# A two-layer transformer on one core: the first feed-forward part's second product by seven products for eight, a fourth raw weight buffer, and token sums held until h

## The chip, the cores and the metric

One core of a Trainium2 chip runs the whole forward pass. The metric is device time in microseconds (us), as the median of several runs of one launch. Engine names: PE is TensorE, DVE is VectorE, ACT is ScalarE, POOL is GpSimd, SP is SyncE (here it only issues DMAs).

## The reference, cut to what matters

Each of two layers takes x (512 tokens by 1024) through three steps, each closed by a layer norm: a feed-forward half step, a token mix (three kinds of attention with gates), and a second feed-forward half step. The change lies in the feed-forward parts, of which there are four in all:

```python
def _swiglu(x, w1, w2):
    gt, up = jnp.split(x @ w1, 2, axis=-1)      # w1: 1024 x 5632
    return (jax.nn.silu(gt) * up) @ w2          # w2: 2816 x 1024
...
x = _layer_norm(DN_ALPHA * x + 0.5 * _swiglu(x, ffn1_w1[l], ffn1_w2[l]), ln1_g[l], ln1_b[l])
```

All data are fp32. The kernel gets fp32 accuracy by three matmuls for one: each operand is split into a high part and a rest (ACT copies the high part `hi`, DVE subtracts to get `lo`), and hi·hi, hi·lo and lo·hi are summed in PSUM.

## The kernel before, in words

**Order of the work.** The program is one stream: FFN part 1 (layer 0, first half step), mix, part 2, part 3, mix, part 4. PE and POOL run in the order in which the code is written (`manual_schedule`). DVE, ACT and SP are ordered by a scheduler when the program is built, and run in that fixed order; an instruction that waits holds everything behind it on its engine.

**First product of a part.** The 2816 features are 22 blocks of 128, `f` = 0 to 21. For f from 4 on, `strassen(f, seven(w1, f))` makes gate and up of a block by seven products for eight: 7 products of 12 matmuls of 256 columns, 84 matmuls per f, into the PSUM tiles `pg`, `pu`, `pv`. `seven` loads two raw weight tiles by SP (L422, L423), sums and differences of them go into `ws` (DVE, L429 to L432), which are split like the weights (L438, L439), and a half tile into `dh`, `dl` (L440, L441). `strassen` copies `pg` to `sn` on ACT (L525) in the middle of the block; PE's later matmuls into `pg` wait for that copy. A last DVE operation on `pg` (L537) and a silu on ACT (L473) make h, kept in `ha` (blocks 0 to 17) and `hb` (18 to 21). The raw tiles rotate through the pool `wt`, 3 buffers. The tokens' own sums (`token_sums`, five DVE groups on x, then splits into `th`, `tl`) are made once per part, while blocks 2 and 3 run.

**Second product of a part.** h (512 by 2816) times w2 (2816 by 1024). In parts 2, 3 and 4 `strassen_rows` takes pairs of feature blocks, 9 pairs (`NS = 9`), and makes each pair's eight block products by seven: a first pass of four products (24 matmuls of 512 columns per pair), merges on DVE, then a second pass of three (18 matmuls per pair); the last 4 blocks (`NTAIL`) are plain, 24 matmuls per block. In part 1 `rows_ln` makes all 22 blocks plainly, 24 matmuls of 512 columns per block. The h of a pair is split and summed by `s_parts` (L491 on): single blocks into `sh`, `sl` (ACT L483, DVE L484, 128x256), differences `s` (L495, L498), their split (L483, L484, 128x768: three tiles in one instruction), and a last difference into `ha` (L503).

**Sums of w2.** The seven products need sums of w2's quarters, `ts` with four planes t1 to t4. `weight_sums` builds them in DRAM by software DMAs that POOL issues (L397), 768 KB each, plain copies and copies that add into the target, 8 per group of 3 pairs. They are taken off a queue one at a time by `sums_step`, which first copies one column of some fresh tile on POOL (L408, `pace`) so that a step does not start before that tile exists. Before the change this happens in the mixes only; part 1 has no `ts` (its first entry is `None`). In part 1's first product POOL also copies bias rows (`bvec`, L436), each behind a copy of a column of `ws` (L435).

Of the kernel before, what the change touches and what calls it, by code (L numbers as in the profile page):

```python
# [64 lines left out]
def body(tc, a, out, depth=DEPTH):  # L65
# [37 lines left out]
    peT = const.tile([P, depth, 2, 32], F32, name="peT")  # L103
    stats = [const.tile([P, 8], F32, name=f"st{i}") for i in range(NB)]
    pace = const.tile([P, 48], F32, name="pace")
    pace, pace2 = pace[:, 0:1], pace[0:64, 16:17]

    xh = xtp.tile([P, KD, S], F32R, name="xh")
    xl = xtp.tile([P, KD, S], F32R, name="xl")
# [4 lines left out]


    extra = K()
    extra.pool, extra.n = None, 0

    def wraw(shape=None):
        extra.n += 1  # L120
        if extra.pool and extra.n % 5 < 2:
            return extra.pool.tile([P, KD, P], F32, name="raw", tag="raw", bufs=2)
        return wt.tile(list(shape or [P, KD, P]), F32, name="raw", tag="raw", bufs=3)

    more = K()
    more.pool, more.n = None, 0
# [138 lines left out]

    def strassen_rows(w2, ts, sp, plain, ln, clear, nxt, tmp):


        def acc8():
            return [ps(name="acc") for _ in range(8)]  # L270
# [11 lines left out]
        a1 = acc8()  # L282
        for p in range(NS):
            if p == 2:
                extra.pool = rp
            rb, ra = wraw(), wraw()
            nc.sync.dma_start(flat(rb)[:, 0:512], w2[2 * p * P:(2 * p + 1) * P, 0:512])
            nc.sync.dma_start(flat(rb)[:, 512:1024], ts[:, p, 1024:1536])
            nc.sync.dma_start(flat(ra), ts[:, p, 0:1024])
            sh, sl = sp(p)  # L290
            ub, ua = wsplit(rb), wsplit(ra)
            prods = [(0, 0, ub, lo4), (1, 3, ub, hi4), (2, 1, ua, hi4), (3, 2, ua, lo4)]
            for i, j, w, c in prods[:1] + prods[2:] + prods[1:2] if p == 0 else prods:
                for b in range(2):
                    mm(a1[2 * i + b], (sh[:, j], sl[:, j]), w, b, c, p == 0, p == NS - 1)
# [34 lines left out]
        for p in range(NS):  # L330
            uc, d, dc = weights(p)
            sh, sl = sp(p, True)
            prods = [(0, 1, uc, lo4), (1, 0, uc, hi4), (2, 2, d, dc)]
            for i, j, w, c in prods[2:] + prods[:2] if p == NS - 1 else prods:
                for b in range(2):
                    mm(a2[2 * i + b], (sh[:, j], sl[:, j]), w, b, c, p == 0, False)
            if p in (1, 2):
                merge(p - 1)
        rest = []
        for k in range(2 * NS, KF):  # L340
            rest.append((k, plain(k), wrows(w2, k)))
        extra.pool.release()
        extra.pool = None
        clear()
        nx.pool = pool("nx", reuse_waits="tile")
        ln.scale_rows()
# [31 lines left out]
        return pts  # L378

    NTAIL = 4  # L380
    NS = 9
    NG = 3
    sums = deque()

    def weight_sums(w2):


        ts = dram.tile([P, NS, 2048], F32, name="ts", tag="ts", bufs=3)
        n = NS // NG

        def step(g, i):
            c = slice(n * g, n * g + n)
            v = w2[2 * n * g * P:2 * n * (g + 1) * P].rearrange("(q two p) f -> two p q f", two=2, p=P)
            b11, b12, b21, b22 = (v[j][:, :, 512 * k:512 * k + 512] for j in range(2) for k in range(2))
            t1, t3, t2, t4 = (ts[:, c, 512 * k:512 * k + 512] for k in range(4))
            o, x = ((t1, b11), (t3, b12), (t2, b22), (t1, b12), (t4, b21), (t3, b22), (t2, t1), (t4, t2))[i]
            nc.gpsimd.dma_start(o, x, **({"accum_op": OP.add} if i in (3, 5, 6, 7) else {}))  # L397

        for g in range(NG):
            sums.extend(lambda g=g, i=i: step(g, i) for i in range(8))  # L400
        return ts

    def sums_step(t, psum=False):
# [40 lines left out]
    def token_sums(st):  # L444


        x = st.ha[:, 10:18]
        th, tl = (st.w1p.tile([P, 4, 4, 256], F32R, name=n) for n in ("th", "tl"))
        t = [y[:, i:i + 2].rearrange("p a (b s) -> p (a b) s", b=2) for y, i in
             ((st.hb, 0), (st.hb, 2), (st.ha, 6), (st.ha, 8))]  # L450
        tt = nc.vector.tensor_tensor
        for i in range(0, KD, 2):
            c = slice(i, i + 2)
            tt(x[:, c], xh[:, c].bitcast(F32), xl[:, c].bitcast(F32), op=OP.add)
        p_, q, r_, s_ = x[:, 0:4, 0:256], x[:, 0:4, 256:512], x[:, 4:8, 0:256], x[:, 4:8, 256:512]
        for i, u, v in ((0, q, p_), (1, s_, t[0]), (2, s_, q), (3, r_, t[1])):
            tt(t[i], u, v, op=OP.subtract)
        for i in range(4):
            nc.scalar.activation(th[:, i], t[i], AF.Copy)
            tt(tl[:, i], t[i], th[:, i].bitcast(F32), op=OP.subtract)  # L460
        st.t = [(th[:, i], tl[:, i]) for i in range(4)]

    def ffn(l, w1, w2, which, xap, xa, wts, pend, done_prev, last, nxt, ts):
# [4 lines left out]
        def hpart(f):  # L468
            return (st.ha, st.hb)[f >= NA][:, f - NA * (f >= NA)]

        def evac(f, pg, pu):
            t = st.lnp.tile([P, S], F32, name="t", tag="t", bufs=3)
            nc.scalar.activation(t, pg, AF.Silu)  # L473
            nc.vector.tensor_tensor(hpart(f), t, pu, op=OP.mult)

        made, hs = {}, {}

        def h_parts(k, t):
            parts(t[:, 0], t[:, 1], hpart(k))
            hs[k] = t  # L480

        def parts(hi, lo, x):
            nc.scalar.activation(hi, x, AF.Copy)  # L483
# [24 lines left out]
        def strassen(f, ws):  # L508
            (ug, u1, u2, ud), (t1, t2, t3, t4) = ws, st.t
            ga, pa, pb = ps(name="pg"), ps(name="pu"), ps(name="pv")  # L510
            p_, r_, s_ = [(xh[:, k:k + 4, c], xl[:, k:k + 4, c]) for k, c in ((0, H1), (4, H1), (4, H2))]

            def prod(o, w, k0, x, first=True):
                for k in range(4):
                    hi, lo = w[0][:, k0 + k], w[1][:, k0 + k]
                    vh, vl = x[0][:, k], x[1][:, k]
                    for i, (wx, vx) in enumerate(((hi, vh), (hi, vl), (lo, vh))):
                        nc.tensor.matmul(o, wx, vx, start=first and k == 0 and i == 0, stop=k == 3 and i == 2,  # L518
                                         skip_group_check=True)

            tt = nc.vector.tensor_tensor
            prod(ga[:, H1], ug, 0, p_)
            prod(ga[:, H2], u1, 0, t1, False)
            sn = st.w1p.tile([P, S], F32, name="sn", tag="sn", bufs=2)
            nc.scalar.activation(sn, ga, AF.Copy)  # L525
# [12 lines left out]
            evac(f, ga, u)  # L538

        pts = staged(wts, pend)  # L540
        for tb in range(NB):
# [7 lines left out]
        st.ha = fa.tile([P, NA, S], F32, name="ha")  # L549
        st.w1p = nx.w1 = pool("w1p", side="right", reuse_waits="tile")  # L550
        more.n = 4
        evac(0, pts[0], pts[1])
        evac(1, pts[2], pts[3])
        for f in range(2, KF):
            if f == KF - 1 and ts is None:
                for k, n in enumerate(("hi", "lo")):
                    h_parts(k, wt.tile([P, KD, P], F32R, name=n, tag=n, bufs=3)
                            .rearrange("p (a b) c -> p a (b c)", a=2))
            elif f == KF - 1:
                w = [wt.tile([P, KD, P], F32R, name=n, tag=n, bufs=3).rearrange("p (a b) c -> p a (b c)", a=4)  # L560
                     for n in ("hi", "lo")]
                v, sn = (st.w1p.tile([P, 2, 256], F32, name=n, tag=n, bufs=2) for n in ("v", "sn"))
# [18 lines left out]
        ln = LN(hsp, which, l, xa, 0.5, last, ts is not None)  # L581

        def wload(k):
            if k not in hs:
                h_parts(k, hsp.tile([P, 2, S], F32R, name="hs", tag="hs", bufs=6))
            return wrows(w2, k)

        def pair():
            return [hsp.tile([P, 4, 256], F32R, name=n, tag=n, bufs=4) for n in ("sh", "sl")]
# [20 lines left out]
            r = [ln.row(n) for n in "GB"]  # L610
            return [[t[:, 0:S] for t in v]] + [[t[:, 0:S], t[:, S:D]] for t in r]

        if ts is None:
            wts, pend = rows_ln(KF, wload, lambda k: hs[k][:, 0], lambda k: hs[k][:, 1], ln, NA, fa.release, nxt)
        else:
            wts, pend = strassen_rows(w2, ts, sp, plain, ln, fa.release, nxt, tmp)

        def done():
            nx_close()
# [903 lines left out]
        tables(*tabs)  # L1523
        init.release()
    wts = pre
    ts = [None]
    for l in range(depth):
        fin = l == depth - 1
        wts, pend, done, xap, xa = ffn(l, a["ffn1_w1"][l], a["ffn1_w2"][l], 0, xap, xa, wts, pend, done, False,
                                       lambda: mix_first(l), ts.pop(0))  # L1530
        ts += [weight_sums(w) for w in [a["ffn2_w2"][l]] + ([] if fin else [a["ffn1_w2"][l + 1]])]
# [34 lines left out]
```

## Time and profile before

| | |
|---|---|
| median of 3 runs | 2469.55 us (2467.5 to 2469.88) |
| the profiled execution's own time | 2472.68 us |
| its span | 2470.9 us |
| busy in the span: PE, DVE, ACT, POOL | 2443.8, 1763.6, 1171.5, 328.0 us |
| part 1: first product's block f = 4 to f = 21 | 63.90 to 247 us |
| part 1: second product | 248.07 to about 370 us |
| first matmul of the second product in parts 2, 3, 4 | 1141.90, 1481.62, 2355.16 us |

The span runs from the first to the last instruction; the execution's time is 1.8 us longer. Lines of the trace give start and length of an instruction, the engine, the line of the kernel, the operation with the tile written and the tiles read, and, in square brackets, how long the engine was idle before it and what ended the wait. PE is busy nearly all the time, so time is won or lost where PE has fewer matmuls or waits.

### The profile page before, as it was taken

The numbers are of one execution on the slowest core, as the hardware profiler recorded it, in microseconds if no ns is written. First come the engines' busy times: TensorE is split into PE (matmuls) and PEld (weight loads), VectorE is DVE, ScalarE is ACT, GpSimd is POOL, SyncE is SP. The second block draws the span as 40 slices with busy tenths as digits, with TensorE's granted clock in tenths as the row PEclk, the third lists the DMA queues.
The fourth block names the chain that finished last, engine by engine and source line by source line (L and its number), as shares of the span: only waits on it lengthen the run. The fifth ranks groups of instructions, "written<-read, shape, count | busy, mean of one in ns | idle before, by whom it ended". The sixth has DMA issues, their size and how long they took to land. (4 is left out here: it accounts for less than half of the span.)

```text
span 2470.9 us, 41023 instructions
## 1 busy us (share of the span) xinstructions
PE 2443.8 (99%) x15529; PEld 2157.1 (87%) x15529; DVE 1763.6 (71%) x3554; ACT 1171.5 (47%) x2262; POOL 328.0 (13%) x598
## 2 busy tenths in 40 slices
PE   9999999999999999999999999999999999999998
PEld 8999888788888789999889998877888888899987
DVE  7888355687653367988879889756776543698887
ACT  4444334576632343445534446445766422344463
POOL 2000000144432210000000000001444100000000
PEclk9999999999999999999999999999999999999999
DMA  7345434656579952336633346646655833323463
GB/s 207 104 120 143 140 96 127 183 152 146 127 209 237 251 172 82 103 104 210 203 98 99 104 144 211 186 113 168 157 155 114 227 102 122 112 87 109 131 210 127
DMA packets 411462, 364.07 MB, mean 147 GB/s; under 512 B 19720, under 2 KB 351640, under 8 KB 411264
## 3 DMA queue, kind: packets, MB, share of 16 engines
q1 hardware_dynamic: 381968, 279.92, 38.5%
q0 software_dynamic: 29296, 81.53, 13.2%
q8 instruction: 122, 2.00, 0.3%
q14 instruction: 76, 0.62, 0.1%
HBM read 334.07 MB, written 74.51 MB: 165 GB/s over the span
## 5 line engine op out<-in xcount | busy, mean ns | idle before, releaser
L156 DVE TENSOR_TENSOR lo<-raw,hi 128x1024 fp32r<-128x1024 f32 (+2 forms) x384 | 450.5, 1182 | 384.4 <-ACT hi L155 380.0
L155 ACT ACTIVATE hi<-raw 128x1024 fp32r<-128x1024 f32 (+2 forms) x384 | 390.1, 1023 | 598.5 <-DMA raw<-in_ffn_w_dram 136.3
L176 PE MATMUL pj<-xh,hi 128*128 128x512 f32 (+1 forms) x720 | 267.0, 371 | 0.1
L177 PE MATMUL pj<-xl,hi 128*128 128x512 f32 (+1 forms) x720 | 254.7, 354 | 1.1 <-DVE xl L242 1.1
L178 PE MATMUL pj<-xh,lo 128*128 128x512 f32 (+1 forms) x720 | 254.7, 354 | 0.0
L518 PE MATMUL pg<-xh,hi 128*128 128x256 f32 x864 | 245.0, 284 | 1.6 <-ACT sn L525 1.6
L518 PE MATMUL pg<-xh,lo 128*128 128x256 f32 x864 | 244.5, 283 | 0.0
L518 PE MATMUL pg<-xl,hi 128*128 128x256 f32 x864 | 244.5, 283 | 0.0
L438 ACT ACTIVATE hi<-ws 128x1024 fp32r<-128x1024 f32 x144 | 151.2, 1055 | 159.7 <-DVE ws L430 69.9
L439 DVE TENSOR_TENSOR lo<-ws,hi 128x1024 fp32r<-128x1024 f32 x144 | 175.4, 1221 | 17.8 <-ACT hi L438 17.7
L275 PE MATMUL acc<-hi,sh 128*128 128x512 f32 x450 | 175.4, 390 | 0.0
L275 PE MATMUL acc<-lo,sh 128*128 128x512 f32 x450 | 175.1, 389 | 0.0
L275 PE MATMUL acc<-hi,sl 128*128 128x512 f32 x450 | 175.1, 389 | 0.0
L518 PEld LDWEIGHTS pg<-xh,hi 128*128 128x128 f32 x864 | 165.8, 192 | 2.7 <-ACT sn L525 2.5
L518 PEld LDWEIGHTS pg<-xl,hi 128*128 128x128 f32 x864 | 165.8, 192 | 0.2
L518 PEld LDWEIGHTS pg<-xh,lo 128*128 128x128 f32 x864 | 165.8, 192 | 0.0
L518 PE MATMUL pu<-th,hi 128*128 128x256 f32 x576 | 163.0, 283 | 0.0
L518 PE MATMUL pu<-tl,hi 128*128 128x256 f32 x576 | 163.0, 283 | 0.0
L518 PE MATMUL pu<-th,lo 128*128 128x256 f32 x576 | 163.0, 283 | 0.0
L178 PEld LDWEIGHTS pj<-xh,lo 128*128 128x128 f32 x720 | 136.3, 189 | 19.6
L176 PEld LDWEIGHTS pj<-xh,hi 128*128 128x128 f32 x720 | 136.7, 190 | 15.3 <-issue 3.1
L177 PEld LDWEIGHTS pj<-xl,hi 128*128 128x128 f32 x720 | 137.0, 190 | 13.0 <-DVE xl L242 1.6
(368 smaller groups left out, 6259.9 us busy)
## 6 DMA issues: line engine op xcount, KB each, us to landing
raw<-in_ffn_w_dram SPq DMA_DIRECT2D x237, 512.0 KB, 4.0
ts<-in_ffn_w_dram POOLq DMA_DIRECT2D x54, 768.0 KB, 9.1
raw<-in_w_in_dram SPq DMA_DIRECT2D x56, 512.0 KB, 4.1
raw<-in_w_gate_dram SPq DMA_DIRECT2D x48, 512.0 KB, 5.2
raw<-ts SPq DMA_DIRECT2D x39, 512.0 KB, 4.2
ts<-ts POOLq DMA_DIRECT2D x18, 768.0 KB, 9.5
x_sp<-xa POOLq DMA_DIRECT2D x24, 512.0 KB, 6.1
ks<-hl SPq DMA_DIRECT2D x96, 128.0 KB, 2.4
```

The source lines that it names most:

```text
L155: nc.scalar.activation(hi[:, c], raw[:, c], AF.Copy)
L156: nc.vector.tensor_tensor(lo[:, c], raw[:, c], hi[:, c].bitcast(F32), op=OP.subtract)
L176: nc.tensor.matmul(o, hi[:, k], vh, start=first, stop=False)
L177: nc.tensor.matmul(o, hi[:, k], vl, start=False, stop=False)
L178: nc.tensor.matmul(o, lo[:, k], vh, start=False, stop=last)
L275: nc.tensor.matmul(o, xx[:, t], ww[:, c], start=first and i == 0, stop=last and i == 2)
L438: nc.scalar.activation(hi, x, AF.Copy)
L439: tt(lo, x, hi.bitcast(F32), op=OP.subtract)
L518: nc.tensor.matmul(o, wx, vx, start=first and k == 0 and i == 0, stop=k == 3 and i == 2, skip_group_check=True)
```

## The change

- `strassen_rows` now runs in part 1 too, with 6 pairs (`NS` is taken from the sums' shape); blocks 12 to 17 are plain, 18 to 21 remain the tail. `rows_ln` stays for the mix's output product.
- Part 1's sums (2 groups of 3 pairs, 16 transfers) are issued by POOL: one per block for the 12 blocks f = 4, 5, 7, 8, ... 20, each paced by h of the block before, and four in the first pass of the second product, each paced by a pair's `sh`. For all sums the order is new: steps 0 to 5 of every group, then 6 and 7 (plane t4) of every group.
- In the first product of every part the pool `lnp` gives a fourth raw weight buffer; in the second product it stays in use beside `rp`, 6 buffers in all for 5. The silu's result goes into a tile `v` of `w1p` (2 buffers, or the tile that the block already has) instead of `lnp`'s `t` (3 buffers).
- `token_sums`' first additions multiply by a column `one` that POOL writes after it has copied a column of h's first block, so that they cannot be placed earlier than h.

```diff
+    pace, pace2, one = pace[:, 0:1], pace[0:64, 16:17], pace[:, 32:33]
...
+    extra.pools, extra.n = [], 0
+    def wraw():
+        seq = [(wt, 3)] * 3 + [(p, n) for p, n in extra.pools for _ in range(n)]
         extra.n += 1
-        if extra.pool and extra.n % 5 < 2:
-            return extra.pool.tile([P, KD, P], F32, name="raw", tag="raw", bufs=2)
-        return wt.tile(list(shape or [P, KD, P]), F32, name="raw", tag="raw", bufs=3)
+        pl, n = seq[extra.n % len(seq)]
+        return pl.tile([P, KD, P], F32, name="raw", tag="raw", bufs=n)
...
+        NS = ts.shape[1]
...
             sh, sl = sp(p)
+            sums_step(sh[:, 0].bitcast(F32))
...
+        for k in range(2 * NS, KF - NTAIL):
+            x, w = plain(k), wrows(w2, k)
+            for tb in range(NB):
+                for hf in range(2):
+                    mm(accs[tb][hf], x, w, tb, slice(4 * hf, 4 * hf + 4), tb >= 2 and hf == 1 and k == 2 * NS, False)
...
-            o, x = ((t1, b11), (t3, b12), (t2, b22), (t1, b12), (t4, b21), (t3, b22), (t2, t1), (t4, t2))[i]
+            o, x = ((t1, b11), (t3, b12), (t2, b22), (t1, b12), (t3, b22), (t2, t1), (t4, b21), (t4, t2))[i]
...
+        for r in (range(6), range(6, 8)):
+            for g in range(ns // n):
+                sums.extend(lambda g=g, i=i: step(g, i) for i in r)
...
+        nc.gpsimd.tensor_copy(pace, st.ha[:, 0, 0:1])
+        nc.gpsimd.memset(one, 1.0)
-            tt(x[:, c], xh[:, c].bitcast(F32), xl[:, c].bitcast(F32), op=OP.add)
+            nc.vector.scalar_tensor_tensor(x[:, c], xh[:, c].bitcast(F32), one, xl[:, c].bitcast(F32), op0=OP.mult,
+                                           op1=OP.add)
...
-            t = st.lnp.tile([P, S], F32, name="t", tag="t", bufs=3)
+            t = st.w1p.tile([P, S], F32, name="v", tag="v", bufs=2) if t is None else t
...
+        extra.pools.append((st.lnp, 1))
...
-            if f == KF - 1 and ts is None:
-                for k, n in enumerate(("hi", "lo")):
-                    h_parts(k, wt.tile([P, KD, P], F32R, name=n, tag=n, bufs=3)
-                            .rearrange("p (a b) c -> p a (b c)", a=2))
-            elif f == KF - 1:
+            if f >= 4 and f % 3:
+                sums_step(hpart(f - 1))
+            if f == KF - 1:
...
-        if ts is None:
-            wts, pend = rows_ln(KF, wload, lambda k: hs[k][:, 0], lambda k: hs[k][:, 1], ln, NA, fa.release, nxt)
-        else:
-            wts, pend = strassen_rows(w2, ts, sp, plain, ln, fa.release, nxt, tmp)
+        wts, pend = strassen_rows(w2, ts, sp, plain, ln, clear, nxt, tmp)
...
-    ts = [None]
+    ts = [weight_sums(a["ffn1_w2"][0], 6)]
```

The scheduler places DVE's work anew. On DVE, where the second product of part 3 begins (the first row is the last operation on `pg`; `lo<-raw` is the split of a weight tile, `hb<-t` is h of block 21, `sl` and `s` belong to pairs 1 on, the row with 128x768 is pair 1's), the program before has:

```order
L537 TENSOR_TENSOR pg<-pg,v 128x256
L495 TENSOR_TENSOR s<-ha 128x512 x2
L156 TENSOR_TENSOR lo<-raw,hi 128x1024
L498 TENSOR_TENSOR s<-ha,s 128x256
L474 TENSOR_TENSOR hb<-t,hb 128x512
L484 TENSOR_TENSOR sl<-ha,sh 128x256
L498 TENSOR_TENSOR s<-ha,s 128x256
L484 TENSOR_TENSOR sl<-ha,sh 128x256 x3
L503 TENSOR_TENSOR ha<-ha,s 128x256
L484 TENSOR_TENSOR sl<-s,sh 128x768
```

At the same place on DVE, right behind the operation on `pg`, the changed program has (its lines are five further on):

```order
L156 TENSOR_TENSOR lo<-raw,hi 128x1024
L483 TENSOR_TENSOR hb<-v,hb 128x512
L500 TENSOR_TENSOR s<-ha 128x512 x2
L489 TENSOR_TENSOR sl<-ha,sh 128x256
L503 TENSOR_TENSOR s<-ha,s 128x256
L489 TENSOR_TENSOR sl<-ha,sh 128x256 x2
L503 TENSOR_TENSOR s<-ha,s 128x256
L489 TENSOR_TENSOR sl<-ha,sh 128x256
L508 TENSOR_TENSOR ha<-ha,s 128x256
L156 TENSOR_TENSOR lo<-raw,hi 128x1024
L508 TENSOR_TENSOR ha<-ha,s 128x256
L489 TENSOR_TENSOR sl<-s,sh 128x768
```

The split of the weight tile has moved ahead of the two differences `s`, and a second split of a weight tile and a second `ha` now stand ahead of the 128x768 row. Parts 1 and 4 have the same rows; part 2 has the first of these moves without the second.

On POOL, from part 1's last block to the layer norm of its second product, the program before has only the four loads of x between the last `bvec` row and the first `st` row. The changed program has, behind the pace and sum of block 20 (`hi` and `sh` are h parts of pairs 0 to 3, `ts` the sums):

```order
L583 DMA xa0_2922<-x_sp_91 128x1024
L583 DMA xa1_2923<-x_sp_91 128x1024
L583 DMA xa2_2924<-x_sp_91 128x1024
L583 DMA xa3_2925<-x_sp_91 128x1024
L414 COPY pace_88<-hi_2781 64x1
L402 DMA ts_201<-in_ffn1_w2_dram 128x3x512
L414 COPY pace_88<-sh_2989 64x1
L402 DMA ts_201<-ts_201 128x3x512
L414 COPY pace_88<-sh_3038 64x1
L402 DMA ts_201<-in_ffn1_w2_dram 128x3x512
L414 COPY pace_88<-sh_3087 64x1
L402 DMA ts_201<-ts_201 128x3x512
```

Four sum transfers, two copies and two additions, now stand behind the loads of x in POOL's order; SP's loads of plane t4 for pairs 0 and 2 of the second pass wait for the second and the fourth of them.

More of the change, by code (lines that the diff above doesn't have):

```diff
@@ L105, in body @@
     pace = const.tile([P, 48], F32, name="pace")
-    pace, pace2 = pace[:, 0:1], pace[0:64, 16:17]
+    pace, pace2, one = pace[:, 0:1], pace[0:64, 16:17], pace[:, 32:33]
     xh = xtp.tile([P, KD, S], F32R, name="xh")
@@ L116, in body @@
     extra = K()
-    extra.pool, extra.n = None, 0
-    def wraw(shape=None):
+    extra.pools, extra.n = [], 0
+    def wraw():
+        seq = [(wt, 3)] * 3 + [(p, n) for p, n in extra.pools for _ in range(n)]
         extra.n += 1
-        if extra.pool and extra.n % 5 < 2:
-            return extra.pool.tile([P, KD, P], F32, name="raw", tag="raw", bufs=2)
-        return wt.tile(list(shape or [P, KD, P]), F32, name="raw", tag="raw", bufs=3)
+        pl, n = seq[extra.n % len(seq)]
+        return pl.tile([P, KD, P], F32, name="raw", tag="raw", bufs=n)
     more = K()
@@ L284, in strassen_rows @@
             if p == 2:
-                extra.pool = rp
+                extra.pools.append((rp, 2))
             rb, ra = wraw(), wraw()
@@ L338, in strassen_rows @@
                 merge(p - 1)
+        for k in range(2 * NS, KF - NTAIL):
[3 more added lines that the diff above has]
+                    mm(accs[tb][hf], x, w, tb, slice(4 * hf, 4 * hf + 4), tb >= 2 and hf == 1 and k == 2 * NS, False)
         rest = []
-        for k in range(2 * NS, KF):
+        for k in range(KF - NTAIL, KF):
             rest.append((k, plain(k), wrows(w2, k)))
-        extra.pool.release()
-        extra.pool = None
+        extra.pools.remove((rp, 2))
+        rp.release()
         clear()
@@ L380, in body, with weight_sums @@
     NTAIL = 4
-    NS = 9
-    NG = 3
     sums = deque()
-    def weight_sums(w2):
-        ts = dram.tile([P, NS, 2048], F32, name="ts", tag="ts", bufs=3)
-        n = NS // NG
+    def weight_sums(w2, ns):
+        ts = dram.tile([P, ns, 2048], F32, name="ts", tag=f"ts{ns}", bufs=3 if ns == 9 else 1)
+        n = 3
         def step(g, i):
@@ L395, in step @@
             t1, t3, t2, t4 = (ts[:, c, 512 * k:512 * k + 512] for k in range(4))
-            o, x = ((t1, b11), (t3, b12), (t2, b22), (t1, b12), (t4, b21), (t3, b22), (t2, t1), (t4, t2))[i]
-            nc.gpsimd.dma_start(o, x, **({"accum_op": OP.add} if i in (3, 5, 6, 7) else {}))
-        for g in range(NG):
-            sums.extend(lambda g=g, i=i: step(g, i) for i in range(8))
+            o, x = ((t1, b11), (t3, b12), (t2, b22), (t1, b12), (t3, b22), (t2, t1), (t4, b21), (t4, t2))[i]
+            nc.gpsimd.dma_start(o, x, **({"accum_op": OP.add} if i in (3, 4, 5, 7) else {}))
+        for r in (range(6), range(6, 8)):
+            for g in range(ns // n):
+                sums.extend(lambda g=g, i=i: step(g, i) for i in r)
         return ts
@@ L469, in hpart, with evac @@
             return (st.ha, st.hb)[f >= NA][:, f - NA * (f >= NA)]
-        def evac(f, pg, pu):
-            t = st.lnp.tile([P, S], F32, name="t", tag="t", bufs=3)
+        def evac(f, pg, pu, t=None):
+            t = st.w1p.tile([P, S], F32, name="v", tag="v", bufs=2) if t is None else t
             nc.scalar.activation(t, pg, AF.Silu)
             nc.vector.tensor_tensor(hpart(f), t, pu, op=OP.mult)
[L476 to L480, printed above, removed]
+        made = {}
         def parts(hi, lo, x):
@@ L537, in strassen @@
             tt(ga[:, H2], ga[:, H2], v[:, H1], op=OP.add)
-            evac(f, ga, u)
+            evac(f, ga, u, v)
         pts = staged(wts, pend)
@@ L580, in ffn, with clear @@
         hsp = pool("hsp", side="right", reuse_waits="tile")
[L581 to L586, printed above, removed]
+        def clear():
+            extra.pools.clear()
+            fa.release()
+        ln = LN(hsp, which, l, xa, 0.5, last, True)
         def pair():
@@ L1530, in body @@
                                        lambda: mix_first(l), ts.pop(0))
-        ts += [weight_sums(w) for w in [a["ffn2_w2"][l]] + ([] if fin else [a["ffn1_w2"][l + 1]])]
+        ts += [weight_sums(w, 9) for w in [a["ffn2_w2"][l]] + ([] if fin else [a["ffn1_w2"][l + 1]])]
         wts, pend, done, xap, xa = mix(l, wts, pend, done, xap, xa, lambda: ffn_first(a["ffn2_w1"][l]))
```

## The prediction

> **What bounds the kernel now.** First the page's busy shares, then PE's waits, then the chain of waits.
>
> ```profile
> PE 2443.8 (99%) x15529; PEld 2157.1 (87%) x15529; DVE 1763.6 (71%) x3554; ACT 1171.5 (47%) x2262; POOL 328.0 (13%) x598
> ...
> PE pg L518 <- ACT sn L525: 1.6, 4, 0.7
> ...
> 1303.22 2.88 PE pu L518 x24
> 1307.54 5.76 PE pg L518 x48
> ...
> 1481.78 99.34 PE acc L275 x438
> ```
>
> PE is idle for only 2470.9 - 2443.8 = 27.1 us. A gain must come from fewer matmuls, or from waits of PE; any new wait counts in full. The chain gives the pitches: a matmul of 256 columns 2.88 / 24 = 0.12 us, so a block f of the first product 84 x 0.12 = 10.08 us; one of 512 columns 99.34 / 438 = 0.2268 us. In the feed-forward parts' products PE waits for ACT's `sn` alone. How much that costs is read from the tile `sn`, one copy per block, first and last start, in part 1 and in part 4:
>
> ```profile
> L525 ACT ACTIVATE sn<-pg x18: 587/590/599, 67.0 to 241.1; 128x512 f32<-128x512 f32 x18
> ...
> L525 ACT ACTIVATE sn<-pg x18: 577/590/598, 2176.8 to 2348.2; 128x512 f32<-128x512 f32 x18
> ```
>
> The 17 steps take 171.4 us in part 4, which is 17 x 10.08, and 174.1 us in part 1: 2.7 us lost there. The timeline of ACT and the waits of SP's queue (150 to 240 us) show why:
>
> ```profile
> 191.38 1.06 ACT L155 ACTIVATE hi<-raw 128x1024 fp32r<-128x1024 f32 x1 [2.50 <-DMA raw<-in_ffn_w_dram]
> 192.34 0.58 ACT L473 ACTIVATE t<-pg 128x512 f32<-128x512 f32 x1
> 192.82 0.59 ACT L525 ACTIVATE sn<-pg 128x512 f32<-128x512 f32 x1
> ...
> SPq L422 <- DVE ws L432: 49.0, 7, 7.3
> SPq L423 <- DVE dl L441: 19.3, 7, 2.8
> ```
>
> ACT's order has a weight split ahead of silu and `sn`; the split waits 2.50 us for its raw tile, and SP issued that load late since it waited for DVE to free one of three buffers.
>
> **The change part by part.**
>
> *Part 1's second product.* Plain it is 22 blocks x 24 = 528 matmuls. Changed: 6 pairs x (24 + 18) + 10 blocks x 24 = 492. 36 x 0.2268 = **8.2 us less**, on PE's path.
>
> *Fourth raw buffer.* With four, a load waits for the block before last, one block of 10.08 us earlier; the longest wait quoted is 7.3 us, so the buffer is free in time. The 2.7 us go: **-2.7**. What is late next would be DVE, which also waits for `ws`; here is its load in part 1:
>
> ```profile
> 154.00:234.00 80.00, 78.35 (x646) 77.50 (x645) 69.24 (x110) 36.47 (x50) 5.09 (x10) 1.00 0.45 121
> ```
>
> 69.24 of 80 us busy leave DVE 10.08 x 10.76 / 80 = 1.4 us per block. POOL's copy of `ws` now stands in two of three blocks behind a pace copy and a sum's issue, 0.6 + 1.25 at most by the rows further down, and `ws` comes free that much later. That is more than 1.4 in the worst case, but not carried over, as every third block has no sum; I take nothing, and 2.7 as the other end.
>
> *DVE's order at the start of the second product* (the two order lists above). PE's order there: pair 0, 24 matmuls, pair 1's first product, 6, then the next, whose second matmul reads the 128x768 `sl`: the 32nd, 31 x 0.2268 = 7.03 us after the first. The trace of part 3:
>
> ```profile
> 1481.62 0.40 PE L275 MATMUL acc<-hi 128*128 128x512 f32 x1
> ...
> 1481.70 1.06 ACT L155 ACTIVATE hi<-raw 128x1024 fp32r<-128x1024 f32 x1 [4.70 <-PE pg L518]
> ...
> 1482.16 1.29 DVE L495 TENSOR_TENSOR s<-ha 128x512 f32<-128x512 f32 x2
> 1483.36 1.22 DVE L156 TENSOR_TENSOR lo<-raw,hi 128x1024 fp32r<-128x1024 f32 x1
> 1484.50 0.42 DVE L498 TENSOR_TENSOR s<-ha,s 128x256 f32<-128x256 f32 x1
> 1484.83 0.69 DVE L474 TENSOR_TENSOR hb<-t,hb 128x512 f32<-128x512 f32 x1
> 1485.44 0.42 DVE L484 TENSOR_TENSOR sl<-ha,sh 128x256 fp32r<-128x256 f32 x1
> ...
> 1487.45 0.95 DVE L484 TENSOR_TENSOR sl<-s,sh 128x768 fp32r<-128x768 f32 x1
> ```
>
> Before, that `sl` ends at 1488.40, 6.78 us after the first matmul: 0.25 us to spare. In the changed order the split of the weight tile comes first, and ACT's half of it ends at 1482.76, 1.14 us after the first matmul, held by PE as before (4.70 us). DVE, free since 0.54, has nothing else that may run. From there, by start-to-start steps of the rows above: split 1.14, `hb` 0.61, two `s` 1.20, then seven steps of 128x256 (four `sl`, two `s`, one `ha`) of 0.33, in all 1.14 + 1.14 + 0.61 + 1.20 + 2.31 = 6.40. In part 2 the 128x768 follows, 0.95: 7.35, so PE waits 0.3. In parts 1, 3 and 4 another split (1.14) and `ha` (0.33) come first: 6.40 + 1.47 + 0.95 = 8.82, so PE waits 1.8. Together 3 x 1.8 + 0.3 = **+5.7 us**; PE has no slack behind it in which that could be made up. Ends: 0, if PE needs that `sl` later than I count, and 4 x 1.8 = 7.2, if part 2 loses as much as the others.
>
> *POOL's copies beside DVE.* In part 1 four pace copies and transfers now stand where DVE is late. What one copy costs DVE:
>
> ```profile
> 205.69 0.69 DVE L431 TENSOR_TENSOR ws<-raw 128x512 f32<-128x512 f32 x1
> 206.29 0.69 DVE L430 TENSOR_TENSOR ws<-ws,raw 128x512 f32<-128x512 f32 x1
> 207.02 0.69 DVE L432 TENSOR_TENSOR ws<-raw,ws 128x512 f32<-128x512 f32 x1
> ...
> 206.44 0.58 POOL L435 COPY pace<-ws 128x1 f32<-128x1 f32 x1 [9.83 <-DVE ws L431]
> ```
>
> The step from 206.29 to 207.02 is 0.73, the one before it 0.60, and the copy lies in it: it held DVE up by 0.13. Two copies in that stretch: **+0.3**. [...]
>
> *The sums of part 1.* Twelve transfers lie in the first product, 10 to 20 us apart. The last four are a chain: copy, addition, copy, addition, the first held by the loads of x until about the second product's start (S). What a transfer takes, and POOL's own work around it:
>
> ```profile
> ts<-in_ffn_w_dram POOLq DMA_DIRECT2D x54, 768.0 KB, 9.1
> raw<-ts SPq DMA_DIRECT2D x39, 512.0 KB, 4.2
> ts<-ts POOLq DMA_DIRECT2D x18, 768.0 KB, 9.5
> ...
> 844.59 0.64 POOL L408 COPY pace<-t 64x1 f32<-64x1 f32 x1
> 851.25 1.25 POOL L397 DMA_DIRECT2D ts<-ts  x1 [6.02 <-DMA ts<-in_ffn_w_dram]
> ...
> DMA to landing us min/median/max: 2.6/5.9/16.9
> ```
>
> The addition waits for its copy's landing (the 6.02). The second copy may start when the first addition is issued, 2.1 us of POOL's work later (1.25 and the next pace copy), and the last addition when that has landed: 9.1 + 2.1 + 9.1 + 9.5 = S + 29.8. SP loads t4 for pairs 2 and 3 then (4.2); ACT's and DVE's splits (1.06, 1.14) stand in DVE's order ahead of the merge that frees the PSUM bank of the second pass's third product. With two more DVE steps (0.95, 0.61) the bank is free 8.0 later, S + 37.8. PE comes there after 6 x 24 + 15 = 159 matmuls, 36.1, plus its 1.8 + 0.3: S + 38.2. Just in time; I take **+0.5** for the spread. Ends: 0, and with all three landings at the longest 16.9, 52.8 + 8.0 - 38.2 = 22.6. [...]
>
> *At nothing:* `token_sums` held by `one` lies beside PE's blocks 2 and 3; the other parts' sums move among themselves in the mixes, beside PE's work; the silu's tile has two buffers for three, and in the Strassen blocks it is one that the block has anyway.
>
> Sum: -8.2 - 2.7 + 5.7 + 0.3 + 0.5 = **-4.4 us**. The profiled execution is 2472.68 (span 2470.9 and 1.8 around it), 3.1 above the median; the terms are differences, so the median 2469.55 becomes 2465.1.
>
> **The rivals.**
>
> *A. DVE's new order costs PE nothing.* Then -10.4, 2459.2. For: no view of before shows PE waiting there, and the margin of 0.25 was read from ends of DVE, not from a wait. Against: every DVE row there follows the one before without a gap.
>
> *B. The sums come too late (slower).* Place: DVE's split of t4 for pairs 2 and 3, in front of the merge in part 1's second pass, with PE's PSUM bank behind it. The chain is in time up to S + 30.2; 4.9 us later the kernel is no faster than before, 9.8 us later slower by over 0.2%, which takes three landings of (40.0 - 2.1) / 3 = 12.6 us each. At 13 the chain ends at S + 41.1, PE waits 10.9, and the whole is -4.9 + 10.9 = +6.0, 2475.6. For: the first pass loads raw tiles all the time, and the longest landing is 16.9. Against: the median.
>
> *C. The fourth buffer doesn't do what it is for.* In part 1 POOL frees `ws` later, DVE is late by what it gained, and `sn` stays behind a late split: 2.7 not won, -1.7, 2467.8. For: 1.4 us of slack against up to 1.85 of new work ahead of the copy. Against: one block in three has none.
>
> **How the numbers follow.** Forecast 0.45, A 0.25, C 0.20, B 0.10. About 0.2% (4.9 us) is what a measurement of this kernel can tell from no change: below 2464.6 is faster, above 2474.5 slower. The forecast lies half a microsecond from that bound; with 2 us of spread I give 0.20 of its 0.45 to faster and 0.25 to the same. Faster 0.20 + 0.25 = 0.45; same 0.25 + 0.20 = 0.45; slower 0.10. The forecast's own range is 2462 to 2468. The range for 8 in 10 takes in A with 1 us to spare and C with the sums partly late (3 more): 2458 to 2471; B is left out.
>
> **What would show it.** Right: in part 1 the 18 `sn` span 171.4 us; its second product has 492 matmuls; PE shows waits of `acc` for `sl` of 1.8, 0.3, 1.8 and 1.8 us in the four parts; the last addition lands near S + 30, with no wait on the second pass's third product. Wrong: no wait for `sl` (A), a wait of many us for a merge in part 1 (B), `sn` still spanning over 173 us (C), or new waits of PE in the mixes, for which no term is here.

## The result and the profile after

The changed kernel takes 2493.55 us in the median of 5 runs (2485.8 to 2498.36), the one before 2469.88 (5 runs, 2467.5 to 2473.53): 1.0091 times as long, 95% interval 1.007 to 1.0112. The forecast was 2465.1. The profiled execution of the changed kernel is its fastest, 2485.8, with a span of 2483.9; the two traces differ by 13.0 us, of the 23.7 between the medians.

First the page's busy shares, then PE's waits from 60 to 330 us, which is part 1, then PE's wait for `sl` over the whole span:

```profile
PE 2439.8 (98%) x15493; PEld 2154.7 (87%) x15493; DVE 1800.1 (72%) x3604; ACT 1198.8 (48%) x2280; POOL 351.2 (14%) x638
```

```profile
PE pg L523 <- ACT sn L530: 8.6, 3, 4.7
PE acc L276 <- DVE B L310: 4.2, 1, 4.2
PE acc L276 <- DVE sl L489: 1.8, 1, 1.8
```

```profile
PE acc L276 <- DVE sl L489: 5.5, 4, 1.8
```

PE has 36 matmuls fewer. Against that stand three new waits. The wait for `sn`, which the fourth buffer was to remove, grew from 1.6 to 8.6 us and lies wholly in part 1's first product; the merge (`B`) in part 1's second pass waits 4.2; `sl` waits four times. The first of the three waits for `sn` in the timelines of ACT, SP's queue, POOL and PE:

```profile
134.29 0.60 ACT L482 ACTIVATE v<-pg 128x512 f32<-128x512 f32 x1 [0.62 <-DVE pg L542]
141.32 1.06 ACT L155 ACTIVATE hi<-raw 128x1024 fp32r<-128x1024 f32 x1 [6.42 <-DMA raw<-in_ffn_w_dram]
142.28 1.04 ACT L444 ACTIVATE hi<-ws 128x1024 fp32r<-128x1024 f32 x1
143.23 0.58 ACT L530 ACTIVATE sn<-pg 128x512 f32<-128x512 f32 x1
...
132.60 0.37 SPq L428 DMA_DIRECT2D raw<-in_ffn_w_dram  x1
133.20 0.79 SPq L429 DMA_DIRECT2D raw<-in_ffn_w_dram  x1
...
129.05 1.29 POOL L402 DMA_DIRECT2D ts<-in_ffn_w_dram  x1 [0.30 <-issue]
129.97 1.07 POOL L442 DMA_DIRECT2D bvec<-bsml  x1
...
140.70 0.28 PE L523 MATMUL pv<-th,dl 128*128 128x256 f32 x1
143.86 0.38 PE L523 MATMUL pg<-xh,hi 128*128 128x256 f32 x1 [2.87 <-ACT sn L530]
...
145.51 0.41 PE L523 MATMUL pg<-xh,hi 128*128 128x256 f32 x1
145.72 0.41 PE L523 MATMUL pg<-xl,hi 128*128 128x256 f32 x1
```

The load issued at 132.60 reaches ACT only at 141.3, 8.6 us later, while a sum (129.05), a bias copy and the second raw tile are under way. ACT's order has the split of that tile ahead of `sn`, as before; so `sn` is late and PE stands still. The tile itself is not urgent: counted by blocks it belongs to f = 13, whose matmuls begin at 158.4, while the `sn` behind it is that of f = 11. Behind the wait comes a second cost: from 145.3 on PE's matmuls start 0.21 us apart for 0.12. The windows have the granted clock in the column behind the engines:

```profile
140.00:144.00 4.00, 1.13 (x10) 0.93 (x9) 1.59 (x2) 2.68 (x4) 0.00 (x0) 1.00 1.11 219
144.00:148.00 4.00, 4.00 (x24) 4.00 (x25) 4.00 (x8) 1.38 (x2) 1.05 (x2) 0.65 0.57 142
```

The clock is 0.65 in the 4 us behind the wait. The three waits for `sn` are gaps of 3.03, 1.25 and 4.83 us in PE's starts, 9.1 in all, and the matmuls behind them that start later than their pitch lose another 1.6, 0.1 and 2.3 us. In part 1's second product the waits for `sl` and for the merge (gaps of 1.94 and 4.37) lose 1.8 and 1.7 in the same way: 7.5 us of slow clock in part 1.

The chain of sums on POOL, with part 1's second product beginning at S = 257.56:

```profile
257.67 0.76 POOL L402 DMA_DIRECT2D ts<-in_ffn_w_dram  x1
270.34 1.28 POOL L402 DMA_DIRECT2D ts<-ts  x1 [10.29 <-DMA ts<-in_ffn_w_dram]
272.01 0.76 POOL L402 DMA_DIRECT2D ts<-in_ffn_w_dram  x1
284.93 1.23 POOL L402 DMA_DIRECT2D ts<-ts  x1 [11.96 <-DMA ts<-in_ffn_w_dram]
```

The two copies take over 12 us each, the last addition 8.7: it lands at S + 36.1 for the S + 29.8 forecast. And DVE where `sl` is late in part 1:

```profile
257.77 0.43 DVE L542 TENSOR_TENSOR pg<-pg,v 128x256 f32<-128x256 f32 x1 [1.26 <-PE pg L523]
258.79 1.23 DVE L156 TENSOR_TENSOR lo<-raw,hi 128x1024 fp32r<-128x1024 f32 x1 [0.59 <-ACT hi L155]
259.93 0.68 DVE L483 TENSOR_TENSOR hb<-v,hb 128x512 f32<-128x512 f32 x1
260.53 1.29 DVE L500 TENSOR_TENSOR s<-ha 128x512 f32<-128x512 f32 x2
...
265.56 0.95 DVE L489 TENSOR_TENSOR sl<-s,sh 128x768 fp32r<-128x768 f32 x1
```

It ends at S + 8.95 (forecast 8.82, and 0.3 for POOL's copies on top).

By stages, profiled execution against profiled execution: to the start of part 1's second product +9.5; from there to the mix's first `cum` +1.7 (-8.2 for the matmuls, +9.8 for the waits and the clock behind them); the first mix with part 2's first product -4.2; part 2's second product to part 3's -1.0; part 3's second product to part 4's +5.4; the rest +1.5. Sum 12.9, with rounding.

Part of what the mixes show can be read from PE's waits there. In the first mix the trace of before has waits for the splits of weight tiles (`gate` 1.4 and 1.1, `acc` 0.7 and 0.6, 3.8 us together) and behind two of them one stretch at half clock (822.1 to 825.5 us); the changed kernel's trace has neither. From part 3's second product to part 4's, new waits for `xl` (1.0), `xa` (0.8) and the silu's `v` (0.6) make 2.4 of the 5.4, and `sl` 1.7. The prediction had no term for any of them.

### The profile page after: what moved, and what is told of

The parts are those of the page before. It is cut to its first block, busy times and chain, and to the rows that moved or that the text cites. A ratio compares the mean times of both kernels' runs of the same rounds, so it can differ in the third digit from the quotient of the medians.

```text
span 2483.9 us, 41102 instructions
## 1 busy us (share of the span) xinstructions
PE 2439.8 (98%) x15493; PEld 2154.7 (87%) x15493; DVE 1800.1 (72%) x3604; ACT 1198.8 (48%) x2280; POOL 351.2 (14%) x638
## 4 chain that ended last, share of the span: by engine, by line
PE 85%; DMA 5%; DVE 5%; ACT 2%; issue 2%; POOL 0%; SPq 0%; DVEq 0%; POOLq 0%; ACTq 0%
PE pg L523 15%; PE acc L276 15%; PE pu L523 8%; PE pj L176 5%; PE pj L177 5%; PE pj L178 5%; PE pv L523 4%; DMA raw<-in_ffn_w_dram 3%; PE gate L176 3%; PE gate L178 3%; PE gate L177 3%; PE brp L178 2%; PE brp L176 2%; PE brp L177 2%; PE sN L1076 2%
## 5 line engine op out<-in xcount | busy, mean ns | idle before, releaser
L156 DVE TENSOR_TENSOR lo<-raw,hi 128x1024 fp32r<-128x1024 f32 (+2 forms) x393 | 460.4, 1179 | 311.3 <-ACT hi L155 309.8
L155 ACT ACTIVATE hi<-raw 128x1024 fp32r<-128x1024 f32 (+2 forms) x393 | 398.6, 1024 | 492.4 <-PE acc L276 81.4
L276 PE MATMUL acc<-hi,sl 128*128 128x512 f32 x606 | 237.5, 392 | 5.5 <-DVE sl L489 5.5
L276 PE MATMUL acc<-hi,sh 128*128 128x512 f32 x606 | 237.6, 392 | 4.2 <-DVE B L310 4.2
L276 PE MATMUL acc<-lo,sh 128*128 128x512 f32 x606 | 237.5, 392 | 0.6 <-DVE lo L156 0.6
L445 DVE TENSOR_TENSOR lo<-ws,hi 128x1024 fp32r<-128x1024 f32 x144 | 175.1, 1217 | 10.3 <-ACT hi L444 10.1
```

The lines of the kernel that those rows point to most:

```text
L155: nc.scalar.activation(hi[:, c], raw[:, c], AF.Copy)
L156: nc.vector.tensor_tensor(lo[:, c], raw[:, c], hi[:, c].bitcast(F32), op=OP.subtract)
L276: nc.tensor.matmul(o, xx[:, t], ww[:, c], start=first and i == 0, stop=last and i == 2)
L445: tt(lo, x, hi.bitcast(F32), op=OP.subtract)
```

## The experiments

Each is compared with the kernel before on the same chip (medians 2469.5 to 2470.2 in the four sets). Differences from the changed kernel are less certain: they go by its five runs, which spread over 12.6 us. Most start from the changed kernel. The first four take one suspect away each.

**The silu tile.** In the changed kernel the silu of block 21 goes to `v` in the pool `w1p`, which is released right behind block 21; the second product's tiles `s`, `sh`, `sl` are put in its space. So DVE may not write `s` before it has read `v` (`hb<-v`).

```diff
-            evac(f, ga, u, v)
+            evac(f, ga, u, st.lnp.tile([P, S], F32, name="t", tag="t", bufs=1) if f == KF - 1 else v)
```

> The changed kernel, with the silu of block 21 written into a tile of the pool lnp again. Theory on the second product's start: the tile v of block 21 lies in the pool w1p, whose space the differences s take over at once, so DVE may not write s before h of block 21 is made; with v out of the way DVE's rows stand in the order of before, PE's waits for sl (5.5 us in four) fall to 0, and 5 to 8 us come back of the 23.7: 2486 to 2489. Rival: the new order comes from the sixth raw buffer or the held token sums; then the waits for sl stay at 5.5 and the time at 2493. The waits for sn in part 1 (8.6 us) and for the merge (4.2 us) stay in both.

2482.43 us (1.0059, 1.0044 to 1.0074), 11 less than the changed kernel where 5 to 8 were expected; between the two profiled executions it is 2.8, for the waits for the merge, `pt` and `lo` grew by 3.3 us together. The head of PE's waits over the whole span:

```profile
PE pg L523 <- ACT sn L530: 7.5, 4, 4.4
PE acc L276 <- DVE B L310: 5.4, 2, 5.1
PE xT L1507 <- DMA xa<-in_x_dram: 4.5, 1, 4.5
```

`sl` is gone from it, in all four parts. The order in which DVE was built is that of before again, `s` ahead of the weight split. On the waits for `sl` and their cause the theory holds and the rival (buffers, held sums) falls; the time missed the expected 2486 to 2489.

**No sums in part 1.** This one leaves out the 16 transfers and feeds part 1's second product rows of w2 instead of sums.

```diff
-            nc.gpsimd.dma_start(o, x, ...)
+            if ns == 9:
+                nc.gpsimd.dma_start(o, x, ...)
...
+        tv = ts if NS == 9 else w2.rearrange("(q p) f -> p q f", p=P)
```

> The changed kernel without the 16 transfers that make part 1's sums (their pace copies stay); part 1's second product loads rows of w2 of the same shape in their place, so its output is another. Theory contention: the raw loads of part 1's first product take 8 to 10 us where 4 to 5 are usual because sums are in flight; without them the loads take about 5, the waits for sn fall from 8.6 to under 3 us, the merge wait of 4.2 goes, and with the clock lost behind these waits the time is about 2473. Rival release: the loads are issued too late, since DVE frees the raw tiles late in each block; then the waits for sn stay above 6 us and only the merge wait goes: about 2486.

2468.42 us (0.9997, 0.9987 to 1.0008). No wait for `sn`, none for the merge, and the raw loads take 4.2 us in the median (longest 6.3) from 70 to 245 us, where the changed kernel's take 6.2 (9.9); the waits for `sl` stay, 5.5 us in four. That is what contention says, and 5 us less than its figure; but the order of DVE's work is another here as well.

**Plain second product in part 1.**

```diff
-    ts = [weight_sums(a["ffn1_w2"][0], 6)]
+    ts = [None]
...
+        if ts is None:
+            wts, pend = rows_ln(KF, wload, ..., ln, NA, clear, nxt)
```

> The changed kernel with part 1's second product plain as before (528 matmuls, no sums in part 1); the fourth raw buffer, the held token sums and the silu's new tile stay. Theory contention: part 1's waits for sn fall below 3 us, the waits for sl stay in parts 2 to 4 (about 4 us): 2470 to 2474. Rival release: the waits for sn stay above 6: 2479 to 2483. If the fourth buffer did its work alone, the 2.7 us that part 1 lost before would be gone too.

2474.85 us (1.0022, 1.0012 to 1.0033): no wait of PE in part 1, the 2.7 us that part 1 lost before are gone. Parts 2 to 4 wait for `sl` and `sh`, 6.2 us together. So the fourth buffer, with what else was changed in the first product, can do its work; it is undone in part 1 by something that comes with the sums.

**All sums in the first product.**

```diff
-            if f >= 4 and f % 3:
+            if 4 <= f < 20:
                 sums_step(hpart(f - 1))
```

> The changed kernel with all 16 sums of part 1 in its first product, one in each block 4 to 19, none in the second product. Merge wait 4.2 us goes in either case, with the slow clock behind it 6 to 7 us. Theory contention: four more blocks with a sum and a bias copy, so the waits for sn grow from 8.6 to 11 or more, and of the 6 to 7 us half is lost again: about 2490. Rival release: the waits for sn stay: about 2487.

2476.82 us (1.0036, 1.0021 to 1.0051), 17 less than the changed kernel, where 3 to 7 were expected. The merge wait is gone; the waits for `sn` did not grow, 6.8 us in three. Both theories erred: four more transfers in the blocks cost nothing that shows in the time, though the raw loads take 7.0 us in the median from 100 to 245 us for 6.2 in the changed kernel. Between the profiled executions the gain is 11.3.

**The bias copies.** Next suspect: POOL's copies of `ws` and the 16 bias copies, which share blocks with the sums.

```diff
+        for i, h in after:
+            nc.gpsimd.dma_start(bvec[i, h:h + 1], ...)
+        after.clear()
```

> The changed kernel with the 16 copies of bias rows issued in one go behind their source, ahead of part 1's block 4, and none in the blocks. The run without sums has shown that the sums slow the raw loads. Theory a, bytes: the sums alone do it, 768 KB read and written beside 1 MB of weights per block; the bias copies are 192 KB and matter little: waits for sn stay at 6 us or more, time 2490. Theory b, order: POOL's copies of ws hold DVE's next sum, the raw tiles are freed late and both loads of a block start together with the sum; without bias copies the loads start about 4 us earlier, as in parts 2 to 4, and the waits for sn fall below 3 us: about 2481.

2499.89 us (1.0122, 1.0107 to 1.0137). Slower than the changed kernel: PE now waits for the splits of the token sums (`tl` 4.7 us, `th` 2.8), which it does not in the changed kernel, and for `sn` still 6.5. That the copies in one go are what makes those splits late is my estimate, not shown apart. The same with the two cures above:

> Three edits of the changed kernel together: silu tile of block 21 back in lnp (sl waits 0), all 16 sums in blocks 4 to 19 (merge wait 0), bias copies ahead of block 4. Theory a: waits for sn of 5 to 8 us stay: 2469 to 2473, no better than before. Theory b: waits for sn under 2 us: 2461 to 2464, faster than before.

2494.81 us (1.0104, 1.0089 to 1.0119): `sn` 10.1, `tl` 4.9, `dl` 3.7. Both theories missed it. Without bias copies in the blocks the raw loads did become short, 3.9 us in the median in the second run (longest 9.7, from 100 to 245 us) for 6.2 (9.9) in the changed kernel, which speaks for theory b. But in these two programs ACT has the silu ahead of `sn`, and the silu waits for DVE, as here in the second run:

```profile
132.31 0.60 ACT L482 ACTIVATE v<-pg 128x512 f32<-128x512 f32 x1 [2.77 <-DVE pg L542]
132.81 0.59 ACT L530 ACTIVATE sn<-pg 128x512 f32<-128x512 f32 x1
```

So `sn` is late in another way, and how much the bias copies hold the loads back stays open. The third run of this kind has both cures again, and the bias copies three at a time in every third block:

```diff
-        if after:
+        if after and f % 3 == 0:
...
+            for i, h in after[:3]:
```

> As combo, but the bias copies three at a time in every third block, 6 to 21, each behind one copy of ws. Theory a: as combo or 1 to 3 us worse where a sum meets three bias copies: 2470 to 2475. Theory b: DVE's sums are held in every third block only: between the run with bias copies in each block and combo, 2465 to 2468.

2466.24 us (0.9986, 0.9976 to 0.9996), 3.7 us faster than before. PE's waits from 60 to 330 us, and how long its raw loads took (70 to 245 us):

```profile
PE pg L524 <- ACT sn L531: 2.2, 1, 2.2
PE acc L276 <- DVE lo L156: 0.5, 1, 0.5
```

```profile
DMA to landing us min/median/max: 2.6/5.6/10.1
```

The loads are about as slow as in the changed kernel (6.2, longest 9.9), yet PE waits 2.2 for 8.6: a slow load is not yet a wait. Is it the bias copies' place, or the two cures? Each without the other:

> The changed kernel with one edit: the bias copies three at a time in every third block, which has no sum. Theory place: a sum, a bias copy and two raw loads at once made the loads late, so apart the waits for sn fall from 8.6 to 3 us or less; the waits for sl (5.5) and the merge (4.2) stay: 2480 to 2485. Rival order: how far a slow load reaches PE depends on how the scheduler has placed DVE's sums in each program, and the 2.2 us of combo_apart came from that; then the waits for sn stay at 6 to 9: 2489 to 2494.

2492.07 us (1.0092, 1.0075 to 1.0108): `sn` 4.3, but `dl` 3.1 and `dh` 2.9, 10.3 in all. Moving the bias copies alone wins nothing that these runs can tell.

> Two edits of the changed kernel: silu tile of block 21 back in lnp, all sums in blocks 4 to 19; bias copies as in the changed kernel. If the causes add up, sl 0, merge 0, sn about 7 us: the run with early sums less 5.5 to 8 us, 2469 to 2471, as fast as before. Rival: the time freed at one place is lost at another, 2475 or more.

2473.56 us (1.0012, 1.0002 to 1.0021): `sl` and merge 0, `sn` 6.1. The two cures add up to a little less than expected; with the bias copies apart 7 us more come back. So their place helps in one program and not in the other.

**The rest of the change.** Three raw buffers, without the line that adds the fourth (and so without the sixth in the second products); and token sums without the hold.

> The changed kernel with three raw buffers in the first products. If the fourth buffer is what took part 1's 2.7 us away in the run with a plain second product, the waits for sn grow from 8.6 to 12 us or more and parts 2 to 4 stay without: 2497 to 2500. Rival, the silu's or the token sums' new place took them away: 2491 to 2495 as the changed kernel.

2500.78 us (1.0124, 1.0109 to 1.0139): part 1's second product starts 11 us later than in the changed kernel. The fourth buffer helps. The wait for `sn` did not grow as expected, it is 5.5 us; PE now waits for the splits of `ws` themselves (`lo` 6.3, `hi` 1.5).

> The changed kernel without the hold on the token sums (plain additions, no copy on POOL). If the hold is neutral, as the prediction took it: 2490 to 2496, waits for sn, sl and merge as in the changed kernel. Rival: without it the additions come ahead of the last xl splits or h's first blocks and PE waits there for 1 us or more per part: 2496 to 2500.

2488.12 us (1.0067, 1.0052 to 1.0082): `sn` 7.6, merge 3.9, `sl` 5.5, about as with the hold. The hold is worth nothing here. The median is 5 us lower than the changed kernel's, but the two intervals overlap (1.0052 to 1.0082, 1.007 to 1.0112) and the profiled executions differ by 1.3 the other way, so a cost of the hold is not shown.

**What the fourth buffer alone is worth:** plain second product and the silu tile in `lnp`.

> Part 1's second product plain, fourth raw buffer, silu tile of block 21 in lnp. What the fourth buffer brings with nothing lost: sn waits 0, sl waits 0, 2.7 us less than before in part 1: 2465 to 2468. Against the three-edit kernel with bias copies apart (2466.2), which has 8.2 us fewer matmuls, it tells what the seven products in part 1 are worth in the end: 8 us if the sums cost nothing (then this one at 2474), about 0 if their transfers eat it.

2465.83 us (0.9982, 0.9973 to 0.9991), the lowest median of all, with no wait of PE from 60 to 330 us, and no seven products in part 1. The 2466.24 above lies within its noise.

**Bytes or order?** To that kernel three things were added: the 12 pace copies alone; with 12 transfers of half the width; with whole ones. Nobody reads what they write.

```diff
     ts = [None]
+    weight_sums(a["ffn1_w2"][0], 6)
```

For the copies alone and for the half width, the step of part 1's sums has two more lines each:

```diff
+            if ns == 6:
+                return
```

```diff
+            if ns == 6:
+                o, x = o[:, :, 0:256], x[:, :, 0:256]
```

> The run with a plain second product in part 1, fourth raw buffer and silu tile in lnp (2465.8), plus only the 12 pace copies on POOL in blocks 4 to 20, without any transfer. Theory bytes: nothing waits, waits for sn 0, 2464 to 2468. Rival order: the copies alone, through POOL's order with the bias copies and DVE's new placement, bring waits for sn of 3 us or more: 2470 or more.

> As dose_pace, with 12 transfers of half the width (384 KB) behind the copies; nobody reads what they write. Theory bytes: raw loads up to 7 or 8 us, waits for sn of 0 to 4 us with the slow clock behind them: 2466 to 2471. Rival order: the same as dose_pace and dose_full.

> As dose_half with the full 768 KB per transfer, as in the changed kernel; nobody reads what they write, and the matmuls are those of the plain second product. Theory bytes: the longest raw load near 10 us, waits for sn of 6 to 12 us and 1 to 4 us of slow clock: 2473 to 2482. Rival order: waits as in dose_pace.

2466.46 (0.9988, 0.9979 to 0.9998), 2471.39 (1.0007, 0.9998 to 1.0016) and 2479.66 us (1.0043, 1.0028 to 1.0058). How long the raw loads took in part 1 (70 to 245 us), copies alone:

```profile
DMA to landing us min/median/max: 3.7/4.3/6.0
```

Half transfers, and PE's wait in part 1:

```profile
DMA to landing us min/median/max: 3.7/5.4/8.2
```

```profile
PE pg L529 <- ACT sn L536: 3.1, 1, 3.1
```

Whole transfers, and PE's wait in part 1:

```profile
DMA to landing us min/median/max: 3.8/6.2/9.9
```

```profile
PE pg L527 <- ACT sn L534: 8.5, 3, 4.4
```

The changed kernel itself, and the kernel before:

```profile
DMA to landing us min/median/max: 3.4/6.2/9.9
```

```profile
DMA to landing us min/median/max: 3.5/4.9/5.6
```

From half to whole, PE's, POOL's and SP's orders are the same, the bytes double, and the waits go from 3.1 to 8.5. With whole transfers both rows are close to those of the changed kernel, though nothing uses the sums. The two programs are not quite alike: from 145 us on some of DVE's and ACT's rows change places. Up to there all orders are the same, and there stands the cleanest pair. A raw tile loaded at 133.8 lands after 5.6 us with half transfers, 8.2 with whole ones; the split of it on ACT, then PE's `pg` behind `sn`, half first (the view puts the second split's wait down to PE, but its tile landed at 142.1):

```profile
139.56 1.06 ACT L155 ACTIVATE hi<-raw 128x1024 fp32r<-128x1024 f32 x1 [3.42 <-DMA raw<-in_ffn_w_dram]
142.10 0.39 PE L529 MATMUL pg<-xh,hi 128*128 128x256 f32 x1
...
142.19 1.06 ACT L155 ACTIVATE hi<-raw 128x1024 fp32r<-128x1024 f32 x1 [6.03 <-PE pv L527]
144.73 0.58 PE L527 MATMUL pg<-xh,hi 128*128 128x256 f32 x1 [2.48 <-ACT sn L534]
```

So here the bytes lengthen the loads (4.3, 5.4 and 6.2 us in the median, 6.0, 8.2 and 9.9 at the longest), and with the same order that alone makes PE wait (2.48 us at 144.73); the copies alone cost nothing that can be measured (2466.46 for 2465.83 without them, and no wait of PE from 60 to 250 us), and the rival falls. How much of the later waits is DVE's and ACT's order was not separated, and the profiled execution with half transfers, 2475.25, is the slowest of its ten.

**Half as many sums.** Three pairs, one group, sums in every other block, silu tile in `lnp`.

```diff
-    ts = [weight_sums(a["ffn1_w2"][0], 6)]
+    ts = [weight_sums(a["ffn1_w2"][0], 3)]
...
-            if f >= 4 and f % 3:
+            if f >= 4 and f % 2:
```

> The changed kernel with the silu tile in lnp and only 3 pairs in part 1: 510 matmuls for 528 plain and 492 with six pairs, 8 sums, all in every other block of the first product. Theory bytes: half the transfers, so half of the waits for sn (2 to 4 us) against 4.1 us of matmuls saved: 2463 to 2467, as the plain product. Rival: with a block between two sums the loads recover, waits for sn under 1: 2461 to 2463, faster than each kernel so far.

2475.39 us (1.0028, 1.0012 to 1.0044): one wait for `sn` of 4.6 us and 1.9 of slow clock behind it, more than the 4.1 us of matmuls saved. Both theories were too hopeful.

## Why the prediction was wrong

- *36 matmuls, -8.2:* held. From the second product's start to the mix the kernel with both cures and the bias copies apart is 7.3 us shorter than before; its one wait there is 0.5.
- *Fourth raw buffer, -2.7:* **this step failed**, and it decided. "With four, a load waits for the block before last, one block of 10.08 us earlier": the load behind the first wait was issued 1.0 us ahead of the start of a block (132.60; block f = 11 starts at 133.6), where the late ones of before came 0.5 us behind such a start, so the fourth buffer brought 1.5 us and not 10, since DVE's last sum of the raw tile still came late (it ended at 132.57). And the twelve transfers, "10 to 20 us apart", had no price at all: I priced POOL's work on them and not their bytes, beside raw loads on which ACT and then PE wait. The other end that I gave, 2.7 not won, was far too narrow: gaps of 9.1 us and 4.0 of slow clock. That transfers alone lengthen the loads, and that a longer load then makes PE wait, is shown by the runs that add only transfers (longest load 6.0 us without, 8.2 with half and 9.9 with whole ones; PE's waits for `sn` 0, 3.1 and 8.5 us); rival C had the place, `sn` behind a late split, and another cause.
- *DVE's order, +5.7:* right, 5.5 us of waits, 1.8, 0.3, 1.7 and 1.7 for the 1.8, 0.3, 1.8 and 1.8 forecast. But "at nothing" stood the silu's tile, which caused it: it moved into a pool whose space is used again at once. Shown by the run with the tile moved back.
- *POOL's copies, +0.3:* not seen, and the 0.13 it was made from is not shown to be the copy's: in the trace of before the same step of DVE takes 0.72 us at 216.82 and at 1068.72, where POOL runs nothing. The late `sl` ended at S + 8.95 for 8.82 without this term, and 0.09 of that is the first split's later start (S + 1.23 for 1.14). The one copy in the stretch, at 259.67, lies beside that split, whose step to the next row is 1.14 us as forecast.
- *Sums of part 1's second product, +0.5:* mechanism right, size wrong. The medians of 9.1 and 9.5 came from the mixes; here the copies take 12.4 and 12.6, while the loads of x and the first pass's raw tiles are in flight; what share each of these has was not tried. The chain ended at S + 36.1, and PE waited 4.4. That was rival B's place and mechanism; by itself it would not have made the kernel slower.
- *Missing altogether:* the slow clock behind the waits, 7.5 us in part 1. The prediction counted a new wait "in full", which was its length alone.
- *The sum:* 2472.68 + 13.1 = 2485.8 for the profiled execution. That the other four runs lie 5.5 to 12.6 us above it stays open: no trace was taken of them. The clock is not enough to explain it: the run of 2493.99 us has a mean granted clock of 0.996, the profiled one 0.995. The changed kernel's runs spread over 12.6 us, those of the kernel with early sums over 7.7, those of the fastest kernel over 3.4. Why the waits in the mixes come and go, also in kernels with a plain part 1, was not followed either.

Moving the bias copies won 7.3 us in one program (2473.56 to 2466.24) and nothing that can be told in another (2493.55 to 2492.07). That where the scheduler has put DVE's sums in each program decides how a slow load reaches PE is my estimate; no run shows it by itself. In the end seven products in part 1 are worth nothing that can be measured: 2466.2 with them and all cures, 2465.8 without, with 36 matmuls more.

## What to carry to other kernels

Price a transfer that is moved beside a loop by its bytes against the loop's own loads, with the longest landing under such a load and not the median of a calmer stage (here 12.4 and 12.6 us for the median 9.1), and follow the late load to the engine that runs in order (here ACT, which waited 6.42 us for a raw tile with `sn` behind it). Price a wait of TensorE at more than its length: in part 1 four of five cost 1.6 to 2.3 us on top. When a tile changes its pool, ask what is put into that space next; here a scheduler turned the new dependency into another order, 5.5 us of waits, and the order can be read before anything runs.

## What the runs showed of the hardware

All of this is read from this case's traces, the clock from their windows. In part 1 of the changed kernel the granted clock is 0.50 in four stretches, each behind a wait of PE. They begin at 145.23, 220.32, 268.11 and 302.24 us and are 3.41 us long, the second 6.83; from one beginning to the next it is 75.09, 47.79 and 34.13 us, which is 22, 14 and 10 times 3.413 us. Windows cut at that step show PE's busy time in a stretch and the clock in the one behind it, first at the first wait for `sn`, then at the wait for `sl` in part 1 and in part 3:

```profile
141.82:145.23 3.41, 1.37 (x11) 1.38 (x12) 2.82 (x3) 2.50 (x4) 0.00 (x0) 1.00 1.12 218
145.23:148.64 3.41, 3.41 (x18) 3.41 (x17) 3.41 (x8) 1.17 (x2) 1.05 (x2) 0.50 0.39 117
148.64:152.06 3.42, 3.42 (x31) 3.42 (x30) 3.42 (x6) 2.15 (x3) 0.00 (x0) 1.00 0.93 231
...
264.70:268.11 3.41, 1.63 (x8) 1.27 (x8) 3.41 (x5) 1.37 (x2) 0.00 (x0) 1.00 1.02 395
268.11:271.52 3.41, 3.41 (x10) 2.63 (x9) 3.41 (x5) 1.06 (x1) 1.18 (x2) 0.50 0.86 305
...
1493.45:1496.86 3.41, 1.68 (x8) 1.05 (x8) 3.41 (x7) 1.72 (x3) 0.00 (x0) 1.00 1.01 370
1496.86:1500.27 3.41, 3.41 (x16) 2.81 (x15) 3.13 (x4) 2.01 (x2) 0.00 (x0) 1.00 0.85 304
```

In the run with early sums two such windows leave PE idle for 1.30 and 1.27 us, and the clock is 1.00 in both:

```profile
128.82:132.24 3.42, 2.12 (x18) 1.92 (x17) 0.18 (x1) 1.27 (x2) 0.89 (x3) 1.00 1.12 348
132.24:135.65 3.41, 2.14 (x18) 2.14 (x19) 3.41 (x5) 1.74 (x3) 0.00 (x0) 1.00 0.35 127
```

With the traces of before and of the changed kernel cut at that step from 45 to 2450 us, the stretches that were followed by half clock were not idle: PE was busy in them for 0.53 to 1.63 us (five, all in part 1 of the changed kernel) and for 1.74 us (one, in the first mix of before, 818.68 to 822.09). All others were followed by the full clock; PE was busy in them for 1.92 us or more, and in one, in part 3, for 1.68. So no single busy time parts the two kinds, and what sets the clock was not shown; a stretch at half clock at 39.42 us of the changed kernel stands behind 3.37 us of PE's work.

At half clock the matmuls start 0.213 us apart for 0.120 (256 columns) and 0.427 for 0.227 (512 columns). So beside its length a wait in part 1 of the changed kernel cost 1.6 to 2.3 us where a stretch at half clock followed, and 0.1 where none did.
